# The last output block of a decoder step in two token halves: second half and samples first, samples stored in four pieces

## The chip, the core and the metric

The kernel runs on one core of a Trainium2 chip. The core has five engines that run at the same time, each with its own queue of instructions: TensorE (PE; its weight loads are listed apart as PEld), VectorE (DVE), ScalarE (ACT), GpSimd (POOL) and SyncE (SP), which here only issues transfers to and from the chip's memory. The metric is the device time of one execution in microseconds, as the median of several runs.

## The reference

One inference step of a one-layer decoder: 256 prompt tokens and 8 x 4 = 32 sample tokens, model width 2048. The layer is two SwiGLU feed-forward parts around a recurrent mixer, each with a norm before and after it:

```python
x = x + 0.5 * rmsnorm(swiglu(rmsnorm(x, g[0]), ffn1_w_in, ffn1_w_out), g[1])
m, sg, sh = hybrid_mixer(rmsnorm(x, g[2]), ...)
x = x + rmsnorm(m, g[3])
x = x + 0.5 * rmsnorm(swiglu(rmsnorm(x, g[4]), ffn2_w_in, ffn2_w_out), g[5])
```

with `rmsnorm(x, w) = x * rsqrt(mean(x*x) + eps) * w` over the 2048 features of a token, and `swiglu(x) = (silu(gate) * up) @ w_out`, hidden width 5632. Only the last line's end matters here: the last part of `@ w_out`, the norm `g[5]`, the residual sum and the stores of `y_prompt` (256 x 2048) and `y_sample` (32 x 2048), all fp32.

## The kernel before

Activations stand with features on the 128 partitions and the T = 288 tokens (256 prompt, then 32 samples) in the free dimension: 16 tiles `x[k]` (the residual) and `y[k]` (the sub-layer's output). Every product is made three times, from a high and a low part of both operands (`wh`, `wl` of the weights; `hh`, `hl` of the hidden activations): `wh*hh`, `wh*hl`, `wl*hh`. The parts are typed fp32r. A 128 x 128 piece of weights is the stationary operand, so each matmul instruction has its own weight load, and 288 tokens move through it.

The output projection of the last two hidden chunks (`do_out(c, 2)`, 8 contraction tiles) goes in four blocks `o` = 0..3 of 512 output features. A block is 8 k x 4 f x 3 = 96 products; the first four k go over all four f, then each f is finished by itself and its `ev` runs: VectorE adds the product to `y[k]` (L597), the squares are summed into `acc` (L336, L338, L340), ScalarE scales by the gain into `z` and `zg` (L609, L610), and PE turns tiles to token-major: `by_token` (two 128 x 128 transposes, L573, copied to `zT` by L574) and `samples` (one transpose, L579, of 4 tiles' samples together, to `zS`).

After the last block `finish` makes the norm: `mean_cols` (L347) sums the squares over features by fp32 matmuls with one moving column (two weight loads and two matmul instructions in the trace for each), then a square root (L163) and a reciprocal (L351). Then `y_prompt` is made in eight pieces of 128 tokens x 512 features, five by VectorE (L677) and three by PE and ScalarE (`scale`, L669, L671), each stored by SP (L665), and `y_sample` by one VectorE instruction (L687) and one store on ScalarE's queue (L688). Half of the residual is turned ahead (`xT`); the other half is turned at the end into PSUM banks (`turned`, L654).

Instructions of an engine are put in order when the kernel is built, by a list scheduler: the first in program order among those that it takes to be ready. At run time each engine's queue is strictly in that order. The weights of the last block have landed and been split before it starts.

Of the kernel before, what the change touches and what calls it, by code (L numbers as in the profile page):

```python
# [9 lines left out]
F32 = mybir.dt.float32  # L10
F32R = mybir.dt.float32r
U8 = mybir.dt.uint8
AF = mybir.ActivationFunctionType
ALU = mybir.AluOpType
PSUM = bass.MemoryType.PSUM

P = 128
TP = 256
TS = 32
T = TP + TS  # L20
NB = 8
ST = 4
D = 2048
KT = D // P
# [103 lines left out]
def trunk(ctx, tc, x_prompt, x_sample, state_gla, state_hgrn, norm_gains, f1_in, f1_out, f2_in, f2_out,  # L128
# [39 lines left out]
    def mmtile(name):  # L168
        return mmp.tile([P, 512], F32, name=name, tag="mm")

    def auxtile(name):
        return aux.tile([P, 512], F32, name=name, tag="aux")
# [15 lines left out]
    def ffn_ops():  # L188

        ops = [("in", 0, 1)]  # L190
        for c in range(1, NCH - 1):
            ops += [("in", c, 1), ("out", c - 1, 1)]
        return ops + [("in", NCH - 1, 1), ("out", NCH - 2, 2)]
# [149 lines left out]
    def mean_cols(ms, parts, c0, c1, start):  # L343

        for i, part in enumerate(parts):
            for t, toks in enumerate(part):
                ins = PE.matmul(ms[:, c0 + t:c0 + t + 1], toks, onesD[:, 0:1], start=start and i + t == 0,  # L347
                                stop=i == len(parts) - 1, skip_group_check=True).ins
        rc = colp.tile([P, c1 - c0], F32, name="rc", tag="rc")
        act(rc, ms[:, c0:c1], AF.Sqrt, bias=epst)  # L350
        V.reciprocal(rc, rc)  # L351
        return rc, ins
# [46 lines left out]
    class Fill:  # L399
# [19 lines left out]
        def products(self, mm, ps):  # L419

            self.ps = auxtile(self.name)
            n = 0
            for dst, parts in ((ps, self.tiles[0]), (self.ps[:, 0:T], self.tiles[1])):
                for k in range(EARLY):
                    for ready in mm(dst, k, parts[k], dst is not ps and k == EARLY - 1):
                        with ExitStack() as es:
                            if n >= 2:
                                es.enter_context(tc.issue_after(self.mean))
                            ready()
                        n += 1  # L430
                        if n == 8:
                            self.go()
# [80 lines left out]
    def ffn(tag, gcol, gnext, pn, before, fill=None):  # L513
# [3 lines left out]
        with ExitStack() as pools:  # L517
# [52 lines left out]
            def by_token(src, k, dst, _, group):  # L570
                tp = auxtile("tp_f")
                for t in range(2):
                    PE.transpose(tp[:, t * P:(t + 1) * P], src[:, t * P:(t + 1) * P], ident)  # L573
                S.activation(dst[:, :, k * P:(k + 1) * P], tp[:, 0:TP].rearrange("p (t c) -> p t c", c=P), AF.Copy)  # L574

            def samples(j, _, dst, group):

                tp = auxtile("tp_s")
                PE.transpose(tp[:, 0:P], group[:, j, :], ident)  # L579
                S.activation(dst[:, j * P:(j + 1) * P], tp[:, 0:P], AF.Copy)  # L580

            def do_out(c, n):
                hs = [hid.pop(c + i) for i in range(n)]
                if final:
                    zt, xt = final_tiles
                end = c + n == NCH
                if end:
                    act_set(AF.Sqrt)
                    if not final:
                        border[0].fill.old()  # L590
                for o in range(4):
                    def ev(f, ps):
                        k = 4 * o + f
                        if c == 0:
                            S.activation(y[k], ps, AF.Copy)
                        else:
                            V.tensor_tensor(y[k], ps, y[k], op=ALU.add)  # L597
                        if end:
                            m = KT - 1 if final else KT - 2
                            sq = sq_add(y[k], k, 0, m - 1, m)  # L600
                            if k >= m:
                                lasts.append(sq)
                            if not final:
                                border[0].fill.new(k)
                            else:
                                if k > 1:
                                    by_token(zs.pop(0), k - 2, *zt)
                                z = fp.tile([P, TP], F32, name="z", tag="u", bufs=3)
                                S.activation(z, y[k][:, 0:TP], AF.Copy, scale=gcol(k))  # L609
                                S.activation(zt[2][:, f, o * TS:(o + 1) * TS], y[k][:, TP:T], AF.Copy, scale=gcol(k))  # L610
                                zs.append(z)
                                if o == 3 and f:
                                    samples(f - 1, *zt)
                    block(f"out{tag}_{c}_{o}", 4 * n, lambda k: [t[:, k % 4, :] for t in hs[k // 4]], ev,
                          tail=2 if end and o == 3 else 1, hold=end and o == 3)
                    k = 4 * (c - 4) + o
                    if final and 0 <= k < KT:
                        G.tensor_copy(xt[2][:, k % 4, k // 4 * TS:(k // 4 + 1) * TS], x[k][:, TP:T])
                        if k >= KT - 4:
                            samples(k % 4, *xt)  # L620
                        if k < X_EARLY:
                            by_token(x[k], k, *xt)

            for kind, c, n in ffn_ops():
                do_out(c, n) if kind == "out" else do_in(c)
            if final:
                zt, xt = final_tiles

                def rest():
                    by_token(zs.pop(0), KT - 2, *zt)  # L630
                    by_token(zs.pop(0), KT - 1, *zt)
                    samples(3, *zt)

                finish(lasts[0][0], rest, zt, xt)
                return None
        return post_norm(gcol, gnext, lasts, f"post{tag}", border[0].fill), border[0]

    def finish(last, rest, zt, xt):

        (zT, zS, _), (xT, xS, _) = zt, xt  # L640
        ms = auxtile("postf")
        rc, _ = mean_cols(ms, [[sq[:, t * P:(t + 1) * P] for t in range(2)] for sq in (acc, last)], 0, 2, True)
        four = []
        for sq in (acc, last):
            r = sqp.tile([P, 4, TS], F32, name="sq4", tag="pn")
            G.tensor_copy(r, sq[:, TP:T].unsqueeze(1).broadcast_to([P, 4, TS]))
            four.append([r.rearrange("p a b -> p (a b)")])
        rest()


        def turned(s, t):
            bank = mmtile(f"yx{s}_{t}")
            for k in range(4):
                PE.matmul(bank[:, k * P:(k + 1) * P], x[4 * s + k][:, t * P:(t + 1) * P], ident, start=k == 0,  # L654
                          stop=False, is_transpose=True, skip_group_check=True)
            return s, t, bank

        banks = [turned(2, 0), turned(2, 1), turned(3, 0)]
        dg = sqp.tile([P, T], F32, name="dg", tag="sq")
        for t in range(2):  # L660
            V.tensor_scalar(dg[:, t * P:(t + 1) * P], ident, rc[:, t:t + 1], None, op0=ALU.mult)

        def store(s, t):
            c = slice(s * 512, (s + 1) * 512)
            nc.sync.dma_start(y_prompt[0, t * P:(t + 1) * P, c], zT[:, t, c])  # L665

        def scale(s, t, bank):
            c = slice(s * 512, (s + 1) * 512)
            ins = PE.matmul(bank, dg[:, t * P:(t + 1) * P], zT[:, t, c], start=False, stop=True,  # L669
                            skip_group_check=True).ins  # L670
            S.activation(zT[:, t, c], bank, AF.Copy)  # L671
            store(s, t)
            return ins

        def add(s, t, x):
            c = slice(s * 512, (s + 1) * 512)
            V.scalar_tensor_tensor(zT[:, t, c], zT[:, t, c], rc[:, t:t + 1], x, op0=ALU.mult, op1=ALU.add)  # L677
            store(s, t)

        add(0, 0, xT[:, 0, 0:512])  # L680
        with tc.issue_after(scale(*banks.pop(0))):
            rcs, _ = mean_cols(ms, four, 2, 3, False)
            own = turned(3, 1)
        add(0, 1, xT[:, 1, 0:512])
        scale(*banks.pop(0))
        add(1, 0, xT[:, 0, 512:])
        V.scalar_tensor_tensor(zS, zS, rcs, xS, op0=ALU.mult, op1=ALU.add)  # L687
        S.dma_start(y_sample.rearrange("b t (q c) -> q (b t) c", q=4), zS)  # L688
        scale(*banks.pop(0))
        add(1, 1, xT[:, 1, 512:])  # L690
        add(*own)

    def mixer(pn, border):
        with ExitStack() as mx:
# [968 lines left out]
```

## Time and profile before

| | us |
|---|---|
| median of 3 runs (lowest to highest) | 2266.38 (2265.66 to 2267.55) |
| the profiled execution's own time | 2263.59 |
| its span, first to last instruction | 2261.8 |
| around the span | 1.79 |
| end of the last product of the output projection, in the span | 2243.49 |
| from there to the span's end | 18.31 |

Times in the rows are microseconds from the span's start. A matmul's listed duration contains the pipeline's depth; what a stream costs is the distance from start to start.

### The profile page before, as it was taken

Reading aid. Unit: us, or ns where it says so; the run is one execution under the profiler, and the core shown is the slowest. Engines: PE = TensorE matmul, PEld = TensorE weight load, DVE = VectorE, ACT = ScalarE, POOL = GpSimd, SP = SyncE. Lnnn points to the kernel's source line nnn. Section 1 sums busy time; section 2 is a strip of 40 time slices with the busy share of each in tenths; the row PEclk is TensorE's granted clock in tenths of the full one; section 3 lists DMA queues with packets and bytes.
Section 4 is the critical chain, followed back from the end, with each engine's and each line's share of the span. In section 5 each row is a group of like instructions: output and inputs, shape, how many; then the busy total and the mean of one; then the engine's idle time right before and its main releaser. Section 6 shows DMA issues by size and latency. Waiting matters only on the chain.

```text
span 2261.8 us, 41302 instructions
## 1 busy us (share of the span) xinstructions
PE 2242.5 (99%) x17063; PEld 2225.7 (98%) x17063; DVE 1361.1 (60%) x2163; ACT 1006.2 (44%) x1507; POOL 80.2 (4%) x144
## 2 busy tenths in 40 slices
PE   9999999999999999999999999999999999999997
PEld 8999999999999999999999999999999999999997
DVE  7545545554565468777888746745555555545554
ACT  6443333333334345455576644543333333334344
POOL 0000000000000003022100000000000000000000
PEclk9999999999999999999999999999999999999999
DMA  6555555555555555466665654555555555555553
GB/s 213 166 167 164 165 167 168 166 162 167 167 167 180 168 167 171 133 209 203 179 171 153 188 177 122 176 163 163 170 168 164 163 168 160 167 168 164 165 166 99
DMA packets 206758, 377.94 MB, mean 167 GB/s; under 512 B 15350, under 2 KB 40164, under 8 KB 206564
## 3 DMA queue, kind: packets, MB, share of 16 engines
q1 hardware_dynamic: 198272, 356.83, 52.2%
q0 software_dynamic: 5984, 17.97, 2.6%
q8 instruction: 135, 2.21, 0.4%
q10 hardware_dynamic: 2308, 0.44, 0.1%
q14 instruction: 59, 0.48, 0.1%
HBM read 363.39 MB, written 11.80 MB: 166 GB/s over the span
## 4 chain that ended last, share of the span: by engine, by line
PE 96%; DVE 1%; DMA 1%; ACT 1%; issue 1%; ACTq 0%; DVEq 0%; SPq 0%
PE gate L478 9%; PE gate L480 9%; PE gate L479 9%; PE out L479 8%; PE out L480 8%; PE out L478 8%; PE up L480 8%; PE up L478 8%; PE up L479 8%; PE mo L480 2%; PE mo L478 2%; PE mo L479 1%; PE hfq L478 1%; PE hfq L479 1%; PE hfq L480 1%; PE qk L478 1%
## 5 line engine op out<-in xcount | busy, mean ns | idle before, releaser
L88 DVE TENSOR_TENSOR wl<-raw,wh 128x1024 fp32r<-128x1024 f32 (+1 forms) x674 | 821.4, 1219 | 643.6 <-ACT wh L87 641.1
L87 ACT ACTIVATE wh<-raw 128x1024 fp32r<-128x1024 f32 (+1 forms) x674 | 711.2, 1056 | 1053.9 <-PE gate L479 314.2
L480 PE MATMUL gate<-xh,wl 128*128 128x288 f32 x1660 | 489.5, 295 | 0.0
L479 PE MATMUL gate<-xl,wh 128*128 128x288 f32 x1660 | 489.2, 295 | 0.0
L478 PE MATMUL gate<-xh,wh 128*128 128x288 f32 x1660 | 489.2, 297 | 0.0
L479 PE MATMUL out<-hl,wh 128*128 128x288 f32 x1408 | 415.9, 295 | 0.0
L478 PE MATMUL out<-hh,wh 128*128 128x288 f32 x1408 | 415.4, 295 | 0.0
L480 PE MATMUL up<-xh,wl 128*128 128x288 f32 x1408 | 415.2, 295 | 0.0
L480 PE MATMUL out<-hh,wl 128*128 128x288 f32 x1408 | 415.1, 295 | 0.0
L478 PE MATMUL up<-xh,wh 128*128 128x288 f32 x1408 | 414.8, 295 | 0.3 <-DVE g L537 0.3
L479 PE MATMUL up<-xl,wh 128*128 128x288 f32 x1408 | 415.0, 295 | 0.0
L479 PEld LDWEIGHTS gate<-xl,wh 128*128 128x128 f32 x1660 | 312.2, 188 | 0.8 <-DVE xl L257 0.5
L480 PEld LDWEIGHTS gate<-xh,wl 128*128 128x128 f32 x1660 | 312.1, 188 | 0.0
L478 PEld LDWEIGHTS gate<-xh,wh 128*128 128x128 f32 x1660 | 310.9, 188 | 0.6 <-ACT xh L256 0.2
L478 PEld LDWEIGHTS up<-xh,wh 128*128 128x128 f32 x1408 | 264.2, 188 | 0.7 <-DVE g L537 0.6
L480 PEld LDWEIGHTS out<-hh,wl 128*128 128x128 f32 x1408 | 264.8, 188 | 0.0
L478 PEld LDWEIGHTS out<-hh,wh 128*128 128x128 f32 x1408 | 264.7, 188 | 0.0
L479 PEld LDWEIGHTS out<-hl,wh 128*128 128x128 f32 x1408 | 264.6, 188 | 0.0
L480 PEld LDWEIGHTS up<-xh,wl 128*128 128x128 f32 x1408 | 264.3, 188 | 0.1
L479 PEld LDWEIGHTS up<-xl,wh 128*128 128x128 f32 x1408 | 264.2, 188 | 0.1
L597 DVE TENSOR_TENSOR y<-out,y 128x288 f32<-128x288 f32 x288 | 121.3, 452 | 104.1 <-PE out L480 101.3
L478 PE MATMUL hfq<-xh,wh 128*128 128x288 f32 x256 | 78.0, 305 | 0.0
(368 smaller groups left out, 2392.6 us busy)
## 6 DMA issues: line engine op xcount, KB each, us to landing
raw<-in_ffn_w_in_dram SPq DMA_DIRECT2D x352, 512.0 KB, 3.7
raw<-in_ffn_w_out_dram SPq DMA_DIRECT2D x176, 512.0 KB, 3.7
raw<-in_mix_w_in_dram SPq DMA_DIRECT2D x64, 512.0 KB, 3.7
raw<-in_mix_w_in_dram SPq DMA_DIRECT2D x96, 256.0 KB, 3.4
raw<-in_mix_w_out_dram SPq DMA_DIRECT2D x32, 512.0 KB, 3.7
out_dram<-s POOLq DMA_DIRECT2D x32, 256.0 KB, 3.4
s<-in_state_gla_dram POOLq DMA_DIRECT2D x16, 256.0 KB, 4.5
s<-in_state_hgrn_dram POOLq DMA_DIRECT2D x16, 256.0 KB, 4.2
```

What stands on the lines that cost most here:

```text
L87: i1 = self.nc.scalar.activation(h[:, c], raw[:, c], AF.Copy).ins
L88: i2 = self.nc.vector.tensor_tensor(l[:, c], raw[:, c], h[:, c].bitcast(F32), op=ALU.subtract).ins
L478: yield lambda: PE.matmul(dst, w[0][:, c:c + P], parts[0], start=start, stop=False)
L479: yield lambda: PE.matmul(dst, w[0][:, c:c + P], parts[1], start=False, stop=False)
L480: yield lambda: PE.matmul(dst, w[1][:, c:c + P], parts[0], start=False, stop=stop)
L597: V.tensor_tensor(y[k], ps, y[k], op=ALU.add)
```

## The change

`finish` goes. Block `o` = 3 of the last chunk becomes `last_block`: the same 96 products first for the 160 columns of the second prompt half and the samples, then again for the 128 columns of the first half. Between the two stand the sums of the second half's norm and of the samples' norm. While the first half is computed, the second half's four pieces of 512 features are scaled, added and stored. The samples are then added by one VectorE instruction and stored in four pieces of 32 x 512 on SP's queue. At last come the first half's norm and five pieces (256, 256, 512, 512, 512 features), all by VectorE. The matmuls that scaled by a diagonal (`dg`) go; the transposes of y in this block are made for each half apart, those of the residual are the same.

```diff
                 for o in range(4):
+                    if end and final and o == 3:
+                        last_block(hs)
+                        break
...
-                            m = KT - 1 if final else KT - 2
+                            m = KT if final else KT - 2
...
+            def last_block(hs):
+                (zT, zS, zg), (xT, xS, _) = final_tiles
+                ws, nk = [W.next() for _ in range(4)], 8
+                waiting = [lambda k=KT - 6 + i: by_token(zs.pop(0), k, *final_tiles[0]) for i in range(2)]
+                def products(ps, f, ks, c):
+                    for k in ks:
+                        w, p = ws[k // 2], slice(k % 2 * 512 + f * P, k % 2 * 512 + (f + 1) * P)
+                        rows = [t[:, k % 4, c] for t in hs[k // 4]]
+                        for i, (a, b) in enumerate(((0, 0), (0, 1), (1, 0))):
+                            PE.matmul(ps, w[a][:, p], rows[b], start=k + i == 0, stop=k == nk - 1 and i == 2)
+                def turn_z(z, t, k):
+                    tp = auxtile("tp_f")
+                    PE.transpose(tp[:, 0:P], z, ident)
+                    S.activation(zT[:, t, k * P:(k + 1) * P], tp[:, 0:P], AF.Copy)
+                def ev(t, f, ps, c):
+                    k = KT - 4 + f
+                    V.tensor_tensor(y[k][:, c], ps, y[k][:, c], op=ALU.add)
+                    sq = sqp.tile([P, T], F32, name="sq", tag="sq")
+                    if f < 3 and (t or f < 2):
+                        S.activation(sq[:, c], y[k][:, c], AF.Square)
+                    else:
+                        V.tensor_tensor(sq[:, c], y[k][:, c], y[k][:, c], op=ALU.mult)
+                    if f < 3:
+                        V.tensor_tensor(acc[:, c], acc[:, c], sq[:, c], op=ALU.add)
+                    z = fp.tile([P, P], F32, name="zh", tag="u", bufs=3)
+                    half = slice(t * P, (t + 1) * P)
+                    S.activation(z, y[k][:, half], AF.Copy, scale=gcol(k))
+                    if t:
+                        S.activation(zg[:, f, 3 * TS:4 * TS], y[k][:, TP:T], AF.Copy, scale=gcol(k))
+                    if waiting:
+                        waiting.pop(0)()
+                    waiting.append(lambda: (turn_z(z, t, k), samples(f, *final_tiles[0]) if t else None))
+                    return sq
+                def turned(s, t):
+                    bank = mmtile(f"yx{s}_{t}")
+                    for k in range(4):
+                        PE.transpose(bank[:, k * P:(k + 1) * P], x[4 * s + k][:, t * P:(t + 1) * P], ident)
+                    return bank
+                def add(t, rc, c0, c1, xs):
+                    V.scalar_tensor_tensor(zT[:, t, c0:c1], zT[:, t, c0:c1], rc, xs, op0=ALU.mult, op1=ALU.add)
+                    nc.sync.dma_start(y_prompt[0, t * P:(t + 1) * P, c0:c1], zT[:, t, c0:c1])
+                second, whole = slice(P, T), slice(0, P)
+                ps = [mmtile(f"end1_{f}")[:, 0:T - P] for f in range(4)]
+                for k in range(4):
+                    for f in range(4):
+                        products(ps[f], f, (k,), second)
+                for f in range(4):
+                    products(ps[f], f, range(4, nk), second)
+                    last = ev(1, f, ps[f], second)
+                ms = auxtile("postf")
+                rc, _ = mean_cols(ms, [[sq[:, P:TP]] for sq in (acc, last)], 0, 1, True)
...
+                rcs, _ = mean_cols(ms, four, 1, 2, False)
+                for f in range(4):
+                    p0 = mmtile(f"end0_{f}")[:, 0:P]
+                    products(p0, f, range(nk), whole)
+                    last = ev(0, f, p0, whole)
+                    if f < 2:
+                        add(1, rc, f * 512, (f + 1) * 512, xT[:, 1, f * 512:(f + 1) * 512])
+                    if f == 1:
+                        add(1, rc, 1024, 1536, turned(2, 1))
+                    elif f == 2:
+                        add(1, rc, 1536, D, turned(3, 1))
+                V.scalar_tensor_tensor(zS, zS, rcs, xS, op0=ALU.mult, op1=ALU.add)
+                for q in range(4):
+                    nc.sync.dma_start(y_sample[:, :, q * 512:(q + 1) * 512].rearrange("b t c -> (b t) c"),
+                                      zS[q * TS:(q + 1) * TS, :])
+                rc, _ = mean_cols(auxtile("postf"), [[sq[:, 0:P]] for sq in (acc, last)], 0, 1, True)
+                for f in waiting:
+                    f()
+                banks = [turned(2, 0), turned(3, 0)]
+                for c0, c1 in ((0, 256), (256, 512), (512, 1024)):
+                    add(0, rc, c0, c1, xT[:, 0, c0:c1])
+                add(0, rc, 1024, 1536, banks[0])
+                add(0, rc, 1536, D, banks[1])
...
-                finish(lasts[0][0], rest, zt, xt)
...
-    def finish(last, rest, zt, xt):
...
-        (zT, zS, _), (xT, xS, _) = zt, xt
-        ms = auxtile("postf")
-        rc, _ = mean_cols(ms, [[sq[:, t * P:(t + 1) * P] for t in range(2)] for sq in (acc, last)], 0, 2, True)
...
-        S.dma_start(y_sample.rearrange("b t (q c) -> q (b t) c", q=4), zS)
```

## Rows read from the trace of the kernel before

**Rows 1.** The page: busy time by engine, share of the span, instructions.
```profile
PE 2242.5 (99%) x17063; PEld 2225.7 (98%) x17063; DVE 1361.1 (60%) x2163; ACT 1006.2 (44%) x1507; POOL 80.2 (4%) x144
```

**Rows 2.** Chain that ended last, from 2235: start, us, what.
```profile
2243.35 0.14 PE out L480
...
2249.79 1.13 ACTq L688
...
2250.97 0.60 ACT zT L671
```

**Rows 3.** Stretches after 2244: length, busy by engine, granted clock, DMA share, GB/s.
```profile
2253.00:2253.50 0.50, 0.00 (x0) 0.00 (x0) 0.00 (x0) 0.00 (x0) 0.00 (x0) 0.98 0.31 74
2253.50:2254.00 0.50, 0.00 (x0) 0.00 (x0) 0.00 (x0) 0.00 (x0) 0.00 (x0) 0.50 0.70 156
...
2259.00:2259.50 0.50, 0.00 (x0) 0.00 (x0) 0.00 (x0) 0.00 (x0) 0.00 (x0) 0.50 0.03 12
```

**Rows 4.** SP's issues in order of time: the first and the last of eight stores.
```profile
2246.91 0.37 SPq L665 DMA_DIRECT2D out_dram<-zT  x1
...
2252.33 1.52 SPq L665 DMA_DIRECT2D out_dram<-zT  x1
```

**Rows 5.** Issue to landing (last column) of the first, fourth and last of these stores.
```profile
out_dram<-zT SPq DMA_DIRECT2D x1, 256.0 KB, 2.2
...
out_dram<-zT SPq DMA_DIRECT2D x1, 256.0 KB, 4.4
...
out_dram<-zT SPq DMA_DIRECT2D x1, 256.0 KB, 7.4
```

**Rows 6.** Chain again: the ends of ten products in a row in the last block.
```profile
2240.25 0.13 PE out L480
...
2241.44 0.14 PE out L480
```

**Rows 7.** Transposes on PE inside the last block, in order of time: first and last.
```profile
2230.00 0.44 PE L573 MATMUL tp_f<-ident,z 128*128 128x128 f32 x2
...
2241.63 0.27 PE L579 MATMUL tp_s<-ident,zg 128*128 128x128 f32 x1
```

**Rows 8.** Weight loads in order of time, with little to move behind them (mixer).
```profile
1014.42 0.53 PEld L1340 LDWEIGHTS oz<-sel,it 128*128 128x128 f32 x4
1014.87 0.19 PEld L478 LDWEIGHTS hi<-xh,wh 128*128 128x128 f32 x1
1014.98 0.19 PEld L479 LDWEIGHTS hi<-xl,wh 128*128 128x128 f32 x1
```

**Rows 9.** Weight loads by shape: count, busy us and mean ns of one.
```profile
L480 PEld LDWEIGHTS out<-hh,wl 128*128 128x128 f32 x1408 | 264.8, 188 | 0.0
...
L1340 PEld LDWEIGHTS oz<-sel,it 128*128 128x128 f32 x32 | 4.6, 192 | 0.0
```

**Rows 10.** Weight loads of matmuls that move 128 fp32 columns (mixer).
```profile
1071.09 0.55 PEld L1349 LDWEIGHTS st<-Vh,kd 128*128 128x128 f32 x4
```

**Rows 11.** Products of 288 columns at the program's start, five in a row.
```profile
9.56 0.44 PE L480 MATMUL gate<-xh,wl 128*128 128x288 f32 x1
...
10.53 0.44 PE L478 MATMUL gate<-xh,wh 128*128 128x288 f32 x1
```

**Rows 12.** Timeline after the last product.
```profile
2243.52 0.46 DVE L597 TENSOR_TENSOR y<-out,y 128x288 f32<-128x288 f32 x1 [0.47 <-PE out L480]
...
2244.02 0.46 DVE L338 TENSOR_TENSOR sq<-y 128x288 f32<-128x288 f32 x1
...
2244.60 0.53 PEld L347 LDWEIGHTS postf<-onesD,sq 128*128 128x128 f32 x4
...
2245.25 0.26 ACT L163 ACTIVATE rc<-postf,epst 128x2 f32<-128x2 f32 x1 [0.35 <-PE postf L347]
...
2245.74 0.48 DVE L661 TENSOR_SCALAR dg<-ident,rc 128x128 f32<-128x128 f32 x2
2246.14 2.07 DVE L677 SCALAR_TENSOR_TENSOR zT<-zT,rc,xT 128x512 f32<-128x512 f32 x3
```

More of the change, by code (lines that the diff above doesn't have):

```diff
@@ L611, in ev @@
                                 zs.append(z)
-                                if o == 3 and f:
-                                    samples(f - 1, *zt)
                     block(f"out{tag}_{c}_{o}", 4 * n, lambda k: [t[:, k % 4, :] for t in hs[k // 4]], ev,
@@ L622, in do_out @@
                             by_token(x[k], k, *xt)
+            def last_block(hs):
[49 more added lines that the diff above has]
+                rc, _ = mean_cols(ms, [[sq[:, P:TP]] for sq in (acc, last)], 0, 1, True)
+                four = []
+                for sq in (acc, last):
+                    r = sqp.tile([P, 4, TS], F32, name="sq4", tag="pn")
+                    G.tensor_copy(r, sq[:, TP:T].unsqueeze(1).broadcast_to([P, 4, TS]))
+                    four.append([r.rearrange("p a b -> p (a b)")])
+                rcs, _ = mean_cols(ms, four, 1, 2, False)
[21 more added lines that the diff above has]
+                add(0, rc, 1536, D, banks[1])
@@ L626, in ffn @@
             if final:
[L627 to L632, printed above, removed]
-                finish(lasts[0][0], rest, zt, xt)
                 return None
         return post_norm(gcol, gnext, lasts, f"post{tag}", border[0].fill), border[0]
-    def finish(last, rest, zt, xt):
-        (zT, zS, _), (xT, xS, _) = zt, xt
-        ms = auxtile("postf")
-        rc, _ = mean_cols(ms, [[sq[:, t * P:(t + 1) * P] for t in range(2)] for sq in (acc, last)], 0, 2, True)
[L643 to L687, printed above, removed]
-        S.dma_start(y_sample.rearrange("b t (q c) -> q (b t) c", q=4), zS)
-        scale(*banks.pop(0))
-        add(1, 1, xT[:, 1, 512:])
-        add(*own)
```

## Prediction

> **What bounds the kernel now.** I read the page first: PE is busy for 99% of the span [rows 1], so time can be won only where PE does not work, or by giving PE less. The chain of waits shows where it does not: the last product of the output projection ends at 2243.49, and from there the chain runs through the norm, VectorE's sums, the issue of the samples' store on ScalarE's queue (1.13 us) and a ScalarE copy that waited behind it, to 2251.57 [rows 2]. The half-microsecond stretches show the rest: transfers until about 2259.5, and around 2253 a hole, DMA share 0.31 and 74 GB/s, while SP stood in its last issue for 1.52 us [rows 3, 4]. That store lands 7.4 us after its issue, where the first took 2.2 [rows 5]: 2252.33 + 7.4 = 2259.73. The span ends 2.07 us later, at 2261.8. So the stretch after the last product is 18.31 us. The change can shorten this stretch; everything up to the start of the last block is untouched. The sum is made against the profiled execution: span 2261.8, its time 2263.59, which is 2.79 under the median shown, 2266.38.
>
> **Where the last block starts.** Nine products in a row take 1.19 us, 0.1325 each [rows 6]; 96 take 12.72. Ten transposes stand among them, 0.11 each (two in 0.38 or 0.44, one alone 0.27) [rows 7]: 1.1. That puts the start at 2243.49 - 13.82 = 2229.67.
>
> **Part 1: the products in two halves.** 192 products of 160 or 128 columns replace 96 of 288. The columns are as many as before, but the weight loads double, and before does not show such a product. A load of a 128-wide piece takes 188 ns in the block and 192 in the mixer's fp32 matmuls, so they are one kind of load [rows 9]. In the mixer four loads with only 32 columns to move behind each take 0.53, (0.53 - 0.19)/3 = 0.113 from start to start, and the next two, of fp32r products, start 0.11 apart as well [rows 8]. With 288 columns to move a load hides behind the products; with 160 it does not. Bounds: below, the loads hide and columns alone count: 288 columns at 2.4 GHz (granted clock 1.00) are 0.120, so 0.0125 is overhead; 160 and 128 columns give 0.079 + 0.066 = 0.145 for a pair, 13.92 in all, +1.2 us. Above, 0.120 each, as the loads of matmuls that move 128 fp32 columns stand [rows 10]: 23.04, +10.3. I take 0.112, between the two rows nearest to it, 0.11 and 0.113: 21.50, **+8.8 us**.
>
> The Trainium skill (TensorE: Matmul & The Clock Gate, Back-to-back issue gap) has about 81 ns for a load and a matmul of 128 columns in a stream. By that the 192 would cost an estimated 15.6, +2.8 instead of +8.8; the same page's section on weight loads has columns / 1.2 in ns, 107 here, with which the loads' 0.11 agrees, so I keep to the rows.
>
> **Part 2: what else PE does before its new last product.** Transposes: 2 of the block before, 4 of k = 10 and 11, 4 + 4 of the second half's y and samples, 8 of the residual (`turned(2, 1)`, `turned(3, 1)`), 1 of the first half: 23 instead of 10, 13 x 0.11 = **+1.4**. The second half's sums and the samples' are 8 matmul passes, 0.113 each by their loads: **+0.9**. The sums must wait for VectorE after the second half's last product (evacuation 0.3, squares 0.3, hand-over 0.1); I cost this wait at nothing because the first half's products are ready and can stand ahead of the sums in PE's queue. Without that cover, with the sums ahead, PE idles some 0.7, and every product behind waits with it. Together PE's last product ends 8.8 + 1.4 + 0.9 = 11.1 later, at 2254.6.
>
> **Part 3: the work that moves under the first half's products.** That half takes 96 x 0.112 = 10.8 us on PE. VectorE gives it four evacuations with squares and sums (about 0.9 each) and four sums of 512 (0.69 each, from three in 2.07 [rows 12]): 6.4. SP issues four stores of 0.37 [rows 4], and the samples' four if their VectorE instruction (a row like the others, 0.7) is queued where its inputs are ready, before the last f. All that costs nothing while the products cover it. If the samples' instruction stays behind the last f, it stands on VectorE ahead of the reciprocal and the samples' four issues (4 x 0.43 with the gaps) stand on SP ahead of the first half's five: some +0.7 at the end. No weights are left to load.
>
> **Part 4: the new end, from PE's last product.** By [rows 12], with 128 of 288 columns: VectorE starts 0.03 after the product, evacuates 128 columns (0.27; the two `dg` of that width take 0.48) and squares them (0.04 + 0.27): 0.61. From there to the first sum 0.12 (2244.48 to 2244.60). From the first of four loads to the root 0.65, with two passes fewer 0.42. Root to the next VectorE instruction after the reciprocal 0.49 (2245.25 to 2245.74). `dg` is gone. Two sums of 256 at about 0.45, three of 512 at 0.69: 2.97. To SP's issue 0.08 (2246.83 to 2246.91). The remaining transposes (10 x 0.11) and their copies lie beside the root and the first three sums. Landing: 2.2 for the first store before, 4.4 for the fourth [rows 5]. The new five are 1 MB against 2 MB and come no faster than VectorE makes them, nothing else is on the queues, and the samples no longer go as one transfer on another queue; I take 2.5. Last, the 2.07 that follow the last landing. Sum: 0.61 + 0.12 + 0.42 + 0.49 + 2.97 + 0.08 + 2.5 + 2.07 = **9.26**, instead of 18.31: **-9.05**.
>
> **The sum.** +11.1 - 9.05 = +2.05: span 2263.85, profiled time 2265.6, median 2268.4. That is +0.09%, and about 0.2% (4.5 us) is what a measurement of this kernel can tell from no change. What the stores win is given back by the weight loads.
>
> **Rivals.**
> *A. The loads hide after all.* +1.2 in place of +8.8: total -5.55, 2260.8, faster by 0.25%. For it: in the block loads and products overlap fully. Against: loads with hardly a column behind them still stand 0.11 apart. By the page's 81 ns it would be an estimated -3.95 instead, 2262.4.
> *B. PE falls to half pace.* At the program's start four products take 0.97, 0.2425 each [rows 11], which is 288 columns at 1.2 GHz; after PE stops the granted clock goes from 1.00 to 0.50 [rows 3]. In the new block columns move only half of the time (0.067 or 0.053 of 0.112). If the clock fell there, loads would stretch likewise, 0.11 more for each product: from 25 products on the result is slower by over 0.2%, and over the first half alone it is +10.6, 2279. Against: PE never stands still here, and before the clock fell only some 3 us after it had stopped.
> *C. The last stores queue up.* If the last of the five lands after 4.4 or 7.4 [rows 5] rather than 2.5, the total is +4.0 to +7.0, 2270.4 to 2273.4; above 5.0 it decides for slower. For it: five stores in 3 us come nearly as fast as 256 KB move. Against: those two waited behind the samples' transfer.
> *D. The order is not the one hoped for.* Sums ahead of the first half's products (+0.7) and the samples late (+0.7): the second half's stores are then beside less. +3.5, 2269.9, still within the measurement.
>
> **Chances and range.** The forecast 0.57; A 0.08; B 0.06; C 0.13; D 0.16. The likeliest is 2268.4. The range goes from 2263.5, where loads at about 0.086 would put it, to 2273, C's upper end; it leaves out most of A and B. Faster: A, 0.08. Slower: B, 0.06, most of C, 0.09, and 0.07 from the upper ends of the forecast (0.120 a product) and D: 0.22. The rest, 0.70, is no change.
>
> **What would show it.** In the changed kernel's trace: products of the last block 0.11 apart instead of 0.13, PE's last product near 2254.6; no idle time of PE between the halves; the second half's four stores and the samples' issued before that; five sums from about 1.6 after it, the last store issued about 4.7 after it and landed by 7.2; the span's end 2.07 behind. Wrong if the spacing is under 0.09 or over 0.125, if the granted clock falls before PE's last product, or if the last store takes over 4 to land.

## The result and the profile after

The changed kernel takes 2273.53 us (median of 20 executions, 2267.78 to 2280.43), the kernel before 2265.49 (20 executions, 2263.01 to 2267.84): ratio 1.0037, interval 1.0027 to 1.0047. The change makes the kernel slower, by more than the forecast's 0.1%, and the median lies 0.5 us above the range.

The median describes hardly any execution. Ten of the twenty lie from 2267.78 to 2270.50 (median 2268.8), with a mean granted clock of 0.998 to 0.999; the other ten lie from 2276.56 to 2280.43 (median 2278.95), with 0.992 to 0.994; nothing lies between. The first ten sit on the forecast, 2268.4. The other ten sit on rival B's time, 2279. The same program gives both, so two executions are shown: the profiled one, of the second kind (2277.69, span 2276.0), and one of the first kind from a later profile of the same kernel (2268.15, span 2266.3).

The chain that ended last, changed kernel, first kind (start, us, what; x24 are the 24 products of one of the first half's four tiles, x19 those of the first tile that stand behind the sums):

```profile
2243.54 0.39 PE end L638 x3
2243.97 0.40 PE postf L347 x2
2244.39 0.27 ACT rc L163
...
2244.80 0.58 PE postf L347 x4
2245.37 2.18 PE end L638 x19
...
2251.10 2.63 PE end L638 x24
...
2254.31 2.63 PE end L638 x24
2256.94 0.13 PE tp_f L642
```

The same view, second kind:

```profile
2243.96 3.68 PE end L638 x19
...
2248.09 5.01 PE end L638 x24
...
2254.40 5.01 PE end L638 x24
...
2260.50 5.01 PE end L638 x24
2265.52 0.23 PE tp_f L642
```

24 products take 2.63 us in the one, 0.110 each, and 5.01 in the other, 0.209. The one-microsecond stretches say when it begins (columns as in [rows 3]). First kind, around the seam between the halves (about 2243.5 to 2245.4) and at PE's end:

```profile
2243.00:2244.00 1.00, 0.96 (x10) 0.82 (x9) 0.65 (x2) 0.65 (x4) 0.20 (x1) 1.00 0.00 0
2244.00:2245.00 1.00, 0.84 (x6) 0.72 (x7) 0.28 (x2) 0.55 (x3) 0.29 (x1) 1.00 0.00 0
2245.00:2246.00 1.00, 1.00 (x11) 1.00 (x11) 0.93 (x3) 0.26 (x1) 0.00 (x0) 1.00 0.02 8
...
2256.00:2257.00 1.00, 1.00 (x12) 1.00 (x12) 0.03 (x1) 0.00 (x0) 0.00 (x0) 1.00 0.67 248
```

Second kind, where the seam stands from about 2241.9 to 2243.6:

```profile
2242.00:2243.00 1.00, 0.96 (x10) 0.82 (x8) 0.47 (x2) 0.90 (x5) 0.30 (x1) 1.00 0.00 0
2243.00:2244.00 1.00, 0.84 (x8) 0.72 (x7) 0.69 (x2) 0.24 (x1) 0.00 (x0) 1.00 0.00 0
2244.00:2245.00 1.00, 1.00 (x8) 1.00 (x8) 0.93 (x3) 0.26 (x1) 0.00 (x0) 0.68 0.12 25
2245.00:2246.00 1.00, 1.00 (x7) 1.00 (x6) 0.11 (x1) 0.00 (x0) 0.00 (x0) 0.50 0.67 248
...
2264.00:2265.00 1.00, 1.00 (x7) 1.00 (x7) 0.00 (x0) 0.00 (x0) 0.00 (x0) 0.50 0.00 0
```

Both have the same busy shares at the seam, 0.96 and 0.84. In the second kind the granted clock goes from 1.00 to 0.50 (from 2.4 to 1.2 GHz) within a microsecond behind the seam and is still 0.50 at 2265, though PE is busy without a gap all the way from 2244 on. In the kernel before it fell only after PE's last product [rows 3].

What stands at the seam, PE's timeline of the second kind (brackets: idle time and what ended it):

```profile
2242.25 0.28 PE L638 MATMUL end<-hh,wl 128*128 128x128 f32 x1
2242.56 0.38 PE L347 MATMUL postf<-onesD,sq 128*128 128x1 f32 x2
2242.81 0.31 PE L638 MATMUL end<-hh,wh 128*128 128x128 f32 x1
2242.95 0.28 PE L638 MATMUL end<-hl,wh 128*128 128x128 f32 x1
2243.39 0.58 PE L347 MATMUL postf<-onesD,sq 128*128 128x1 f32 x4 [0.16 <-ACT rc L163]
2243.83 0.30 PE L638 MATMUL end<-hh,wl 128*128 128x128 f32 x1
```

The sums were not queued behind a longer run of the first half's products. They stand among its first five, in PE's queue, three products and then two in front of them. From the third product's start to the sum of `last` are 0.31 us (2242.25 to 2242.56), 0.2 more than the usual 0.11; from the fifth's to the samples' sums 0.44 (2242.95 to 2243.39), 0.33 more. The first wait is for the square of the last tile on VectorE. The second is for ScalarE, whose root `rc` reads the bank `postf` that the samples' sums are to be written into.

### The profile page after: what moved, and what is told of

The parts are those of the page before. It is cut to its first block, busy times and chain, and to the rows that moved or that the text cites. A ratio compares the mean times of both kernels' runs of the same rounds, so it can differ in the third digit from the quotient of the medians.

```text
span 2276.0 us, 41514 instructions
## 1 busy us (share of the span) xinstructions
PE 2260.0 (99%) x17153; PEld 2243.9 (99%) x17153; DVE 1365.2 (60%) x2174; ACT 1006.3 (44%) x1516; POOL 80.3 (4%) x144
## 4 chain that ended last, share of the span: by engine, by line
PE 96%; DVE 2%; issue 1%; ACT 1%; DMA 0%; DVEq 0%; SPq 0%; ACTq 0%
PE gate L478 10%; PE gate L480 10%; PE gate L479 10%; PE up L480 8%; PE up L478 8%; PE out L479 8%; PE up L479 8%; PE out L480 8%; PE out L478 8%; PE mo L480 1%; PE mo L478 1%; PE mo L479 1%; PE hfq L478 1%; PE hfq L479 1%; PE hfq L480 1%; PE end L638 1%
## 5 line engine op out<-in xcount | busy, mean ns | idle before, releaser
L479 PE MATMUL out<-hl,wh 128*128 128x288 f32 x1376 | 406.3, 295 | 0.0
L478 PE MATMUL out<-hh,wh 128*128 128x288 f32 x1376 | 405.6, 295 | 0.0
L480 PE MATMUL out<-hh,wl 128*128 128x288 f32 x1376 | 405.5, 295 | 0.0
L480 PEld LDWEIGHTS out<-hh,wl 128*128 128x128 f32 x1376 | 258.7, 188 | 0.0
L478 PEld LDWEIGHTS out<-hh,wh 128*128 128x128 f32 x1376 | 258.6, 188 | 0.0
L479 PEld LDWEIGHTS out<-hl,wh 128*128 128x128 f32 x1376 | 258.5, 188 | 0.0
```

The costliest lines, as they stand in the source:

```text
L478: yield lambda: PE.matmul(dst, w[0][:, c:c + P], parts[0], start=start, stop=False)
L479: yield lambda: PE.matmul(dst, w[0][:, c:c + P], parts[1], start=False, stop=False)
L480: yield lambda: PE.matmul(dst, w[1][:, c:c + P], parts[0], start=False, stop=stop)
```

## The experiments

Up to four kernels shared a chip and its executions of the kernel before (21 to 31 on each chip, medians 2265.37 to 2265.59). "Fell" counts the executions with a mean granted clock of 0.996 or less: of those 81 executions of before it is one, at 2270.11. Three explanations of the fall stand against each other: narrow products alone; PE's stops at the seam alone; and the seam's one-column sums (eight passes within some 2 us, with hardly a column to move) with narrow products behind them, made more frequent by the stops.

**The changed kernel again**, on two chips.

> The changed kernel once more, for its spread on one chip and for a trace of an execution in which the clock holds. Theory N (narrow products: the columns move only about half of the time in the last block, and this by itself lets the clock fall) and theory S (the seam between the halves, with PE's short stops and one-column sums, lets it fall) both expect the two groups of times seen so far, about 2268.5 and about 2278, each in near half of the executions; in a trace of the lower group PE's last product near 2254.6 and the end 9.3 after it.

> The changed kernel on the same chip as the run with the stops alone, for the share of executions in which the clock falls there: about half (14 of 26 so far).

2278.54 (2268.90 to 2279.24, 6 executions), ratio 1.0043 (1.0027 to 1.0059), 4 of 6 fell; and 2278.68 (2268.15 to 2279.59, 6), 1.0054 (1.0041 to 1.0068), 5 of 6 fell. With the first twenty that is 19 of 32. The clock falls on both of these chips, so it is the kernel, not one chip.

**More columns in the first half**, in both halves, in the second half alone, and 160 instead of 240. The surplus columns are computed and not used.

```
-  p0 = mmtile(f"end0_{f}")[:, 0:P]
-  products(p0, f, range(nk), whole)
-  last = ev(0, f, p0, whole)
+  p0 = mmtile(f"end0_{f}")
+  products(p0[:, 0:240], f, range(nk), slice(0, 240))
+  last = ev(0, f, p0[:, 0:P], whole)
```

> The first half's products move 240 columns instead of 128 (112 of them are computed again and not used), everything else as changed. At full clock a weight load covers 240 columns, so the price is 0 to 0.8 us. Theory N: the second half and the seam are as before, but the wide stream keeps the clock or brings it back, so the upper group goes or shrinks to a few us: median about 2269 to 2271. Theory S: the fall at the seam stays as frequent, and the wide stream brings the clock back after some us: an upper group about 3 to 5 above the lower. Both differ if the clock stays low to the end: then the width of the first half's products does not matter.

> Both halves' products move 240 columns (80 or 112 of them computed again and not used). Price at full clock 0 to 1.5 us (0.112 to 0.120 a product). Theory N: the clock never falls, all executions lie within 2268 to 2271. Theory S: the seam is unchanged, so the clock still falls there in near half of the executions, with an upper group some 3 to 5 us above.

> Only the second half, which stands ahead of the seam, moves 240 columns; seam and first half (128 columns) are as changed. If what PE did just before the seam counts with it, the clock holds, one group near 2269. If the seam and what follows it decide, it falls in about half of the executions, and two groups near 2269 and 2279 remain.

> The first half's products move 160 columns, as the second half's do, instead of 128 (32 computed again and not used); the seam is as changed. Price 0, since a load covers 160 columns. If a little more work in the array after the seam is enough, one group near 2268; if not, two groups as in the changed kernel, perhaps with fewer executions in the upper one.

First half 240: 2269.55 (2267.18 to 2271.56, 11), 1.0019 (1.0010 to 1.0028), 0 of 11 fell. Both halves 240: 2269.55 (2267.79 to 2270.09, 11), 1.0019 (1.0010 to 1.0028), 0 of 11. Second half alone: 2276.69 (2268.55 to 2278.38, 8), 1.0037 (1.0024 to 1.0049), 5 of 8. First half 160: 2269.45 (2266.62 to 2278.71, 11), 1.0023 (1.0013 to 1.0032), 2 of 11 (2278.71 and 2274.46; a third, 2271.39 at 0.997, lies just outside the count). In the first of these kernels the seam is still there: the builder put two products and then one in front of its sums, PE waits there no less than in the changed kernel, and the clock holds. PE's timeline, the sums and then two products nine apart:

```profile
2246.15 0.58 PE L347 MATMUL postf<-onesD,sq 128*128 128x1 f32 x4 [0.22 <-ACT rc L163]
...
2246.79 0.27 PE L638 MATMUL end<-hl,wh 128*128 128x240 f32 x1
...
2247.80 0.27 PE L638 MATMUL end<-hl,wh 128*128 128x240 f32 x1
```

(2247.80 - 2246.79)/9 = 0.112: the 112 unused columns are free, and more columns move in the same time. So the seam by itself, with its stops and its sums, doesn't do it, against theory S: both are there and the clock holds. Wide products before the seam don't hold it (5 of 8 fell); wide products behind it do.

**The seam taken away**: the second half's sums wait until the first of the first half's tiles is done, the samples' until the second is. Nothing is left out.

```
-    rc, _ = mean_cols(ms, [[sq[:, P:TP]] for sq in (acc, last)], 0, 1, True)
...
-    rcs, _ = mean_cols(ms, four, 1, 2, False)
+    last1 = last
     for f in range(4):
...
+        if f == 0:
+            rc, _ = mean_cols(ms, [[sq[:, P:TP]] for sq in (acc, last1)], 0, 1, True)
...
+        if f == 1:
+            rcs, _ = mean_cols(ms, four, 1, 2, False)
```

> Products as narrow as in the change, but the second half's sums go behind the first f of the first half and the samples' sums behind the second, so that PE does not stop between the halves. Price 0, gain about 0.5 us of PE's stops. Theory N: the clock still falls in about half of the executions, two groups at 2268 and 2277. Theory S: it holds in nearly all, one group, median about 2268.

2268.15 (2266.08 to 2269.13, 11), 1.0013 (1.0004 to 1.0022), 0 of 11 fell. The products are as narrow as in the changed kernel, and the clock holds, so narrow products alone don't do it, against theory N. PE runs from the second half into the first without a gap, and the sums wait for nothing:

```profile
2241.65 0.28 PE L638 MATMUL end<-hh,wl 128*128 128x160 f32 x1
2241.88 0.27 PE L579 MATMUL tp_s<-ident,zg 128*128 128x128 f32 x1
2241.91 0.31 PE L638 MATMUL end<-hh,wh 128*128 128x128 f32 x1
...
2244.62 0.33 PE L347 MATMUL postf<-onesD,acc 128*128 128x1 f32 x2
2244.81 0.36 PE L347 MATMUL postf<-onesD,sq 128*128 128x1 f32 x2
2245.21 0.31 PE L638 MATMUL end<-hh,wh 128*128 128x128 f32 x1
```

**Sums at the seam without their waits**: taken over `acc` twice, the samples' in a bank of its own. That leaves the last square out of the second half's and the samples' norms.

```
-  rc, _ = mean_cols(ms, [[sq[:, P:TP]] for sq in (acc, last)], 0, 1, True)
+  rc, _ = mean_cols(ms, [[sq[:, P:TP]] for sq in (acc, acc)], 0, 1, True)
...
-  for sq in (acc, last):
+  for sq in (acc, acc):
...
-  rcs, _ = mean_cols(ms, four, 1, 2, False)
+  rcs, _ = mean_cols(auxtile("postg"), four, 0, 1, True)
```

> As changed, with the sums at the seam still there (8 one-column passes), but made from acc twice, without the last square, and the samples' sum in a bank of its own, so that PE hardly stops at the seam. It leaves the last square of the second half and the samples out of their norms. Theory P (PE's stops at the seam, about 0.5 us, together with the narrow products let the clock fall): it holds, one group near 2268. Theory C (the one-column passes with the narrow products are enough): it still falls in near half of the executions, two groups.

**Stops at the seam without the sums**: the seam taken away as above, and in its place a transpose that waits for the last square and one that waits for ScalarE's copy of it; both results are discarded.

```
   last1 = last
...
+  PE.transpose(st1[:, 0:P], last1[:, P:TP], ident)
...
+  S.activation(sc, st1[:, 0:P], AF.Copy)
...
+  PE.transpose(st2[:, 0:P], sc, ident)
...
```

> The second half's sums late, as in the run before that moved them (there the clock held in 11 of 11), but with two stops of PE put back at the seam: a transpose that waits for the last square and a second one that waits for ScalarE's copy of the first; no one-column pass stands there. If PE's stops of together some 0.5 us with the narrow products are enough, the clock falls in a good part of the executions (two groups, 2268 and 2278); if the one-column passes are needed as well, it holds in nearly all.

Sums without waits: 2268.44 (2266.05 to 2277.27, 12), 1.0018 (1.0008 to 1.0028), 2 of 12 fell. Stops without sums: 2268.97 (2266.55 to 2271.81, 11), 1.0013 (1.0004 to 1.0022), 0 of 11. The latter's timeline shows 0.35 + 0.20 us of idle PE, more than the 0.04 + 0.16 that the two stretches at the changed kernel's seam leave:

```profile
2242.74 0.30 PE L685 MATMUL stop<-ident,sq 128*128 128x128 f32 x1 [0.35 <-DVE sq L652]
...
2243.41 0.33 PE L689 MATMUL stop<-ident,stopc 128*128 128x128 f32 x1 [0.20 <-ACT stopc L687]
```

With the stops alone the clock held each time, where the changed kernel on the same chip fell in 5 of 6; with the sums alone it fell now and then (2 of 12), where theory P had it hold and theory C had it fall in near half; with both together, in 19 of 32. If sums with and without waits let the clock fall equally often, counts as far apart as 19 of 32 and 2 of 12 would come about once in 80 (21 falls dealt at random to 44 executions). That speaks for the third explanation, but weakly where it says that the stops make the fall more frequent. Twelve executions don't measure the smaller rate well; against the one kernel on the same chip that has the seam with its stops and 128 columns behind it, the one with a wide second half, it is 2 of 12 against 5 of 8, which would come about once in 19. And without the waits the passes also stand closer, four, one product, four, so that waits and spacing changed together:

```profile
2244.12 0.50 PE L347 MATMUL postf<-onesD,acc 128*128 128x1 f32 x4
2244.49 0.31 PE L638 MATMUL end<-hh,wh 128*128 128x128 f32 x1
2244.63 0.58 PE L347 MATMUL postg<-onesD,sq 128*128 128x1 f32 x4
```

**The other half of the change alone**: before, with the samples stored in four pieces, on SP, and on ScalarE's queue behind its last copy.

```
-  S.dma_start(y_sample.rearrange("b t (q c) -> q (b t) c", q=4), zS)
+  for q in range(4):
+      nc.sync.dma_start(y_sample[:, :, q * 512:(q + 1) * 512].rearrange("b t c -> (b t) c"),
+                        zS[q * TS:(q + 1) * TS, :])
```

The second kernel issues the same four with `S.dma_start` at the end, ordered after the last of the ScalarE copies.

> The kernel before, with the samples' store alone as in the change: four pieces of 32 x 512 on SP's queue instead of one transfer on ScalarE's. If the one transfer held up the stores queued behind it (the hole around 2253, landings of 7 us), the last store lands 3 to 4.5 us sooner: about 2261.5, 0.15 to 0.2 per cent under before. If the end of before is bound by the 2.4 MB alone, no change.

> The kernel before with the samples in four pieces, but on ScalarE's queue and behind its last copy, so that SP's last three stores don't stand behind four small issues (0.5 us each). If the hole of the four pieces on SP's queue (rates under 200 GB/s for 1.5 us) is what is left to win, the last landing comes about 1 us sooner than with the pieces on SP: 2262, else it stays at 2263.

On SP: 2263.15 (2261.47 to 2265.04, 11), 0.9990 (0.9981 to 0.9999), 2.2 us below before on the same chip; 2261.5 was expected. On ScalarE's queue: 2261.77 (2258.90 to 2263.92, 11), **0.9980** (0.9971 to 0.9989), the fastest kernel of this study, 3.66 us below before on the same chip. The two intervals overlap, so which of the two queues is the better one is not shown. In its profile ScalarE's last copy waits for PE, no longer behind the store's issue; SP's eighth store takes 0.40 us to issue, where it took 1.52 [rows 4], but the seventh now takes 1.22; and the hole of 74 GB/s at a DMA share of 0.31 [rows 3] has become a dip to 148 GB/s at 0.91 (timeline, then the dip's lowest half microsecond):

```profile
2251.95 0.60 ACT L673 ACTIVATE zT<-yx 128x512 f32<-128x512 f32 x1 [0.26 <-PE yx L671]
2252.02 3.35 ACTq L695 DMA_DIRECT2D out_dram<-zS  x4
2253.01 1.22 SPq L665 DMA_DIRECT2D out_dram<-zT  x1
...
2254.32 0.40 SPq L665 DMA_DIRECT2D out_dram<-zT  x1
...
2253.50:2254.00 0.50, 0.00 (x0) 0.00 (x0) 0.00 (x0) 0.00 (x0) 0.00 (x0) 1.00 0.91 148
```

From its last product's end (2245.50, in the chain) to the span's end (2260.0) are 14.5 us instead of 18.31. With the pieces on SP it is 14.4 (2247.63 to 2262.0); why the median there is only 2.2 us below before, no run shows.

## Why the prediction was wrong

**The step that failed** is in Part 2: "I cost this wait at nothing because the first half's products are ready and can stand ahead of the sums in PE's queue". They were ready, but only three and then two of them stood ahead. By the starts in PE's timeline the stops cost about 0.2 + 0.33 = 0.5 us in themselves. With them failed the reason given against rival B, "PE never stands still here, and before the clock fell only some 3 us after it had stopped": here it fell within a microsecond behind a seam with two delays of 0.2 and 0.33, and rival B got 0.06 where 19 of 32 executions went its way. The waits in themselves are a small miss; the clock is the large one, and it takes more than the waits: with stops alone it held in 11 of 11, and the sums, which the prediction counted as +0.9 on PE and nothing else, have to stand there too, with narrow products behind them.

Rival B's time came out right, worked out +10.6 and 2279, measured 2278.95, and in part by luck. It priced 96 products. By the chains the 91 behind the seam took 8.6 us more, (5.01 - 2.63) x 3 = 7.1 in three tiles and 3.68 - 2.18 = 1.5 in the first, and the transposes between them, which it left out, 1.35. The two groups' medians differ by 10.1.

The Trainium skill (TensorE: Matmul & The Clock Gate, HAM oscillation) ties such a fall to idle gaps of TensorE, waits for transfers above all. Here it came without a wait for a transfer: where PE idled for 0.35 and 0.20 us with no sums, the clock held in 11 of 11, and where the sums stood without waits, it fell in 2 of 12.

**The rest of the sum held, but for one more wait.** Of the first kind, by its own trace:

- Part 1, the products: in the second half nine steps take 1.00 us (first and last start below, second kind, before the fall), 0.111 each, at 160 columns; in the first half 0.110; at 240 columns 0.112. Forecast 0.112. The spacing does not follow the columns, as it would if the loads were hidden, so rival A is out.

```profile
2235.01 0.28 PE L638 MATMUL end<-hh,wh 128*128 128x160 f32 x1
...
2236.01 0.28 PE L638 MATMUL end<-hh,wh 128*128 128x160 f32 x1
```

- Parts 1 and 2, the block from its first product to PE's last: 2231.14 to 2256.94, 25.8 us. Read in the same way, the block of before runs from 2229.43 (its first product's start, below; the prediction worked out 2229.67) to 2243.49, 14.06 us, and with the forecast's 11.1 that makes 25.2. The products took 0.3 less than forecast; two waits that the sum has at nothing took 0.9. One is the 0.5 at the seam. The other stands at the head of the block: the transposes of the block before wait for ScalarE's `z`, 0.49 us from the second product's start to theirs (2231.22 to 2231.71), 0.38 more than usual, so PE stood still there too, in every variant with halves, also in those in which the clock always held. Without the seam's sums (second half's and samples' moved), first product to span end takes 34.5 instead of 35.2. Before, then first kind:

```profile
2229.43 0.29 PE L478 MATMUL out<-hh,wh 128*128 128x288 f32 x1
...
2231.14 0.24 PE L638 MATMUL end<-hh,wh 128*128 128x160 f32 x1
2231.22 0.27 PE L638 MATMUL end<-hl,wh 128*128 128x160 f32 x1
2231.71 0.44 PE L573 MATMUL tp_f<-ident,z 128*128 128x128 f32 x2 [0.22 <-ACT z L613]
```

- Part 3: the second half's stores and the samples' pieces are issued while PE works; the last two samples' pieces at 2253.16 (below), before the last tile's products begin (2254.31).
- Part 4, the tail: 2266.3 - 2256.94 = 9.36, forecast 9.26. Timeline and issues, first kind:

```profile
2253.16 0.92 SPq L704 DMA_DIRECT2D out_dram<-zS  x2
...
2256.97 0.29 DVE L647 TENSOR_TENSOR y<-end,y 128x128 f32<-128x128 f32 x1 [1.68 <-PE end L638]
2258.43 0.16 DVE L351 RECIPROCAL rc<-rc 128x1 f32<-128x1 f32 x1 [0.77 <-ACT rc L163]
2258.63 1.54 DVE L672 SCALAR_TENSOR_TENSOR zT<-zT,rc,xT 128x256 f32<-128x256 f32 x3
2260.09 1.40 DVE L672 SCALAR_TENSOR_TENSOR zT<-zT,rc,yx 128x512 f32<-128x512 f32 x2
2261.85 0.41 SPq L673 DMA_DIRECT2D out_dram<-zT  x1
...
out_dram<-zT SPq DMA_DIRECT2D x1, 256.0 KB, 2.7
```

  The first sum begins 1.69 after the product (forecast 1.6), the last issue 4.91 after it (4.7), and the landing takes 2.7 (2.5); the span ends 1.75 behind it (2.07). Rival C is out.
- The sum: first product to span end, 35.16 against 2261.8 - 2229.43 = 32.37 before: +2.79, forecast +2.05. The first kind's ten against before: 2268.8 - 2265.49 = +3.3.

**Where the gain went, when the clock held.** The tail became 9 us shorter, as forecast, and the doubled loads, the added transposes, the sums and the waits took 25.8 - 14.06 = 11.7 on PE. A good part of those 9 had nothing to do with the halves: the four pieces alone shorten the tail from 18.31 to 14.5. Beside the kernel with four pieces the halves save only 14.5 - 9.36 = 5.1 us of tail for those 11.7. The halves with the samples in one transfer were not run; that the halves are the loss follows by subtraction, +3.3 with both parts and the clock held, -2.2 with the pieces alone on SP.

**What stays open.** Why the same program lets the clock fall in one execution and not in the next. The last block's first product starts at 2229.74, 2231.14 and 2231.37 us in the three profiles of the changed kernel, and the clock fell in the first and the last of them, so that does not settle it. How few sums, or how far apart, would be safe was not measured; four behind each of two tiles were (0 of 11).

## What to carry to other kernels

Splitting a matmul's moving side in two doubles its weight loads; where a load takes 0.11 us, products of 128 to 240 columns all take that long, and the split is paid in full on an engine that is the bound (96 products of 0.1325 us became 192 of 0.11). Where a stream of narrow matmuls has to contain small sums that wait for other engines, let them come one group at a time behind a whole tile of products (0 of 11 fell here), and look at the times of many executions: one profile would have told either story here. When an edit has two parts, time each alone: here the small one, four pieces for one store, was the gain, and the large one, by subtraction, the loss.

## What the runs showed of the hardware

The granted clock fell from 1.00 to 0.50 behind a spot with eight one-column passes and delays of PE of 0.2 and 0.33 us, and stayed at 0.50 for some 20 us of gapless work, in which products of 128 columns took 0.209 us each instead of 0.110. With products of 240 columns behind such a seam it fell in 0 of 11 executions, with 160 in 2 of 11, with 128 in 19 of 32; with stops of 0.35 and 0.20 us and no passes, in 0 of 11.

One store of the samples, 256 KB as a transfer whose slowest dimension has four entries, held other stores back: the last one landed after 7.4 us [rows 5]. As four transfers of 32 rows the samples' pieces on SP landed in a median of 2.6 us, and so did the eight stores beside them; with the pieces on ScalarE's queue the last store took 3.7. A long issue is not tied to that one store: 1.52 us before [rows 4], but also 1.22 with the four pieces on ScalarE's queue.
